# Split weights placed first in SBUF, and identity transposes in five chunks of a two-layer encoder kernel

## Chip, cores and metric

The kernel runs on one core of a Trainium2 chip. The metric is the device time of one execution in microseconds. The kernel is given as the median of several runs; one further execution was taken by the hardware profiler, and every trace number comes from that one.

## What is computed

A trunk of two layers over 256 tokens of width 2048, in fp32. Each layer is a norm, a token mixer, a residual add, a norm, a gated MLP with a depthwise convolution of width 3, a residual add. Layer 0 mixes with a bidirectional mLSTM of 8 heads, layer 1 with a bidirectional gated linear recurrence (HGRN2) of 16 heads.

```python
def conv_glu(hn, w_up, conv_w, conv_b, w_down):
    u = hn @ w_up                                   # 2048 -> 2 x 5504
    a, v = jnp.split(u, 2, axis=-1)
    ...                                             # c: a convolved over 3 tokens
    return (jax.nn.gelu(c, approximate=False) * v) @ w_down

def reference(x, ...):
    h = x
    for layer in range(DEPTH):
        hn = rmsnorm(h, norm_mix_g[layer])
        if layer % N_MIXERS == 0:
            mix = mlstm_mixer(hn, ...)              # p = hn @ w_in -> q, k, v, o, gates; y @ w_out
        else:
            mix = hgrn_mixer(hn, ...)               # p = hn @ w_in -> q, i, g, f_f, f_b; y @ w_out
        h = h + mix
        h = h + conv_glu(rmsnorm(h, norm_ffn_g[layer]), ...)
    return rmsnorm(h, final_g)
```

## The kernel before

**Products in three parts.** All large products run on TensorE as fp32r. A weight tile `raw` comes from memory, ScalarE rounds it to `wh` (L144) and VectorE takes the rest, `wl = raw - wh` (L145). Activations are split in the same way; a tile `x` of 128 features holds the high half of 256 tokens in its columns 0 to 255 and the low half in 256 to 511. A product is wh with x high, wh with x low, and wl with x high.

**Chunks.** The whole program is one list of chunks that `stream` works off in order. A chunk is a strip of a weight matrix with all `nk` tiles of the contraction dimension, and accumulates in two PSUM banks `ps`. There are two main kinds:

- "fm" (feature-major, 256 weight columns): the weights are stationary and x moves. For each k and each of the two halves f there is one pair: L199 moves all 512 columns of x past wh, L200 moves the first 256 past wl. A chunk of 16 k has 32 pairs. The q and k projections of the mLSTM, the q and gate projections of the HGRN and the up projections of the MLP are of this kind.
- "tm" (token-major, 512 weight columns): x is stationary and the weights move. For each k and each of the two token halves t there are three products of 512 columns: L189 (x high, wh), L190 (x high, wl), L191 (x low, wh). The v, o, g and all output and down projections are of this kind. L176 to L178 are the same for the very last chunk.

The first chunk mixes both kinds (L189 to L194).

**The order of the chunks.** In the mLSTM, for each of four pairs of heads `pr`: v (tm), q (fm), k (fm), o (tm), and then four chunks of the output projection (tm). The MLP is cut in two parts: 22 up chunks (fm), four down chunks (tm), 21 up chunks (fm), four down chunks (tm). The HGRN has for each of four groups of heads three fm chunks, v, three fm chunks, g, and then its output projection.

**Side work.** The attention parts, and the transposes that bring the residual stream into feature-major form for the next norm (`Norm.turn`, L268), are generators that `Side` steps between the products. Their short matmuls therefore stand among the pairs of the fm chunks. They write to a ring of four PSUM banks, handed out by `aux`. `Norm.turn` runs in the chunks that follow an output projection with a norm behind it: the first up chunk of each layer's first part, and the first chunks of the HGRN. Behind the down projection of a first part nothing is pushed.

**Where tiles lie.** A tile pool takes its place in SBUF in the order in which pools are opened, and its tiles lie in the order in which they are first asked for. `keep` comes first (parameters, constants with the identity `ident`, the residual stream hx, the 16 tiles xt, the 16 tiles yt, which hold ya, yb and g0 to g15 in turn), then `wpool` (three raw, four wh, four wl), then `ev`, and then the pools of the stages; the MLP's pool holds g16 to g21. The instructions are put in order by the tile framework with a timeline model; in both kernels the order on every engine is that of the source but for this scheduling.

Of the kernel before, what the change touches and what calls it, by code (L numbers as in the profile page):

```python
# [9 lines left out]
F32R = mybir.dt.float32r  # L10
# [5 lines left out]
P = 128  # L16
T = 256
D = 2048
KT = D // P
# [24 lines left out]
WB = 4  # L44
# [8 lines left out]
def trunk_kernel(ctx, tc, xT, x_d, fg_d, pp_d, cst_d, w_first, w_aq, w_ak, w_av, w_ao, w_aout,  # L53
                 w_bq, w_bv, w_bg, w_bout, w_up, w_down, out, mscr):
    nc = tc.nc
    act, dve, pool, pe = nc.scalar, nc.vector, nc.gpsimd, nc.tensor

    keep = ctx.enter_context(tc.tile_pool(name="keep", bufs=1))
    wpool = ctx.enter_context(tc.tile_pool(name="wpool", bufs=1))
    ev = ctx.enter_context(tc.tile_pool(name="ev", bufs=1))  # L60
# [11 lines left out]
    ident = cst[:, C_ID:C_ID + P]  # L72
# [5 lines left out]
    def aux(name):  # L78
        return psa.tile([P, 512], F32, tag="aux", name=name)


    class Side:
        def __init__(self):
            self.now, self.jobs = 0.0, []
# [26 lines left out]


    class Chunk:
        def __init__(self, kind, src, nk, x, done, before=None, last=False):
            self.last = last
            self.kind, self.src, self.nk, self.x, self.done, self.before = kind, src, nk, x, done, before
            self.width = {"fm": 256, "tm": 512, "first": 512 + P}[kind]

    def split_weights(chunks):

        first = True
        for ch in chunks:
            total = ch.nk * ch.width
            cuts = [0]
            if first:
                cuts = [k * ch.width for k in FIRST]
            while cuts[-1] < total:
                cuts.append(min(total, cuts[-1] + 2048))
            step = ch.width if first else 1024
            for b0, b1 in zip(cuts, cuts[1:]):  # L130
                n = b1 - b0
                raw = wpool.tile([P, 2048], F32, tag="raw", bufs=RAW, name="raw")
                nc.sync.dma_start(raw[:, :n], ch.src[:, b0:b0 + n])
                if first:
                    k0, k1 = b0 // ch.width, b1 // ch.width
                    (nc.scalar if k0 < 2 else nc.sync).dma_start(hx[:, k0:k1], xT[:, k0:k1])
                    if k0 == 0:
                        nc.scalar.dma_start(pp[:, 0:KT], pp_d[:, 0:KT])
                for c0 in range(0, n, step):
                    m = min(step, n - c0)  # L140
                    wh = wpool.tile([P, 1024], F32R, tag="wh", bufs=WB, name="wh")
                    wl = wpool.tile([P, 1024], F32R, tag="wl", bufs=WB, name="wl")
                    r = raw[:, c0:c0 + m]
                    act.copy(wh[:, :m], r)  # L144
                    dve.tensor_tensor(wl[:, :m], r, wh[:, :m].bitcast(F32), ALU.subtract)  # L145
                    yield wh, wl, m // ch.width
            first = False

    def stream(chunks):
        pieces = split_weights(chunks)  # L150
        ready = []

        def fetch():
            p = next(pieces, None)
            if p is not None:
                ready.append(p)

        for _ in range(LOOK):
            fetch()
        for ch in chunks:  # L160
            if ch.before:
                ch.before()
            ps = [psm.tile([P, 512], F32, tag="mm", name="mm") for _ in range(3 if ch.kind == "first" else 2)]
            k = 0
            while k < ch.nk:
                fetch()
                wh, wl, n = ready.pop(0)
                if ch.last and k + sum(p[2] for p in ready) + n == ch.nk:
                    pieces_, k0 = [(wh, wl, n)] + ready, k
                    for t in range(2):  # L170
                        k = k0
                        for wh, wl, n in pieces_:
                            for kk in range(n):
                                x, c = ch.x(k), slice(kk * 512, (kk + 1) * 512)
                                xh, xl = x[:, t * P:(t + 1) * P], x[:, T + t * P:T + (t + 1) * P]
                                pe.matmul(ps[t], xh, wh[:, c], start=False, stop=False)  # L176
                                pe.matmul(ps[t], xh, wl[:, c], start=False, stop=False)
                                pe.matmul(ps[t], xl, wh[:, c], start=False, stop=k == ch.nk - 1)  # L178
                                k += 1
                        ch.half(ps[t], t)  # L180
                    return
                for kk in range(n):
                    x = ch.x(k)
                    st, sp = k == 0, k == ch.nk - 1
                    if ch.kind != "fm":
                        c = slice(kk * 512, (kk + 1) * 512)
                        for t in range(2):
                            xh, xl = x[:, t * P:(t + 1) * P], x[:, T + t * P:T + (t + 1) * P]
                            pe.matmul(ps[t], xh, wh[:, c], start=st, stop=False)  # L189
                            pe.matmul(ps[t], xh, wl[:, c], start=False, stop=False)  # L190
                            pe.matmul(ps[t], xl, wh[:, c], start=False, stop=sp)  # L191
                        if ch.kind == "first":
                            pe.matmul(ps[2], wh[:, 512:512 + P], x, start=st, stop=False)
                            pe.matmul(ps[2][:, 0:T], wl[:, 512:512 + P], x[:, 0:T], start=False, stop=sp)  # L194
                        side.tick(1.3)
                    else:
                        for f in range(len(ps)):
                            c = kk * ch.width + f * P
                            pe.matmul(ps[f], wh[:, c:c + P], x, start=st, stop=False)  # L199
                            pe.matmul(ps[f][:, 0:T], wl[:, c:c + P], x[:, 0:T], start=False, stop=sp)  # L200
                        side.tick(0.325 * len(ps))
                    k += 1
            ch.done(ps)
# [179 lines left out]
    def mlstm(norm, nxt):  # L383
# [150 lines left out]
        chunks = []  # L534
        for pr in range(AH // 2):
# [41 lines left out]
                chunks.append(Chunk("first", w_first, KT, first_x, done_first, begin))  # L577
            else:
                chunks.append(Chunk("tm", w_av[pr - 1], KT, norm.x, done_v))
            chunks.append(Chunk("fm", w_aq[pr], KT, norm.x, done_q))  # L580
            chunks.append(Chunk("fm", w_ak[pr], KT, norm.x, done_k))
            chunks.append(Chunk("tm", w_ao[pr], KT, norm.x, done_o))

# [196 lines left out]
    def ffn(layer, norm, nxt):  # L780
        stack = ExitStack()
        box = {}
        chunks = []

        def begin():
            box["mp"] = stack.enter_context(tc.tile_pool(name="ff", bufs=1))
            if isinstance(nxt, FinalNorm):
                nxt.begin(box["mp"])

        def done_up(f, i, GT):  # L790
            def go(ps):
                mp, R = box["mp"], norm.R
                a = mp.tile([P, T], F32, tag="a", bufs=2, name="a")
                v = mp.tile([P, T], F32, tag="v", bufs=2, name="v")
                c = mp.tile([P, T], F32, tag="c", bufs=2, name="c")
                fm_scaled(ps[0], R, a)
                fm_scaled(ps[1], R, v)
                cw = [col("conv_w", (layer * 3 + w) * FT + f) for w in range(3)]
                dve.tensor_scalar(c, a, cw[1], col("conv_b", layer * FT + f), ALU.mult, ALU.add)
                dve.scalar_tensor_tensor(c[:, 1:T], a[:, 0:T - 1], cw[0], c[:, 1:T], ALU.mult, ALU.add)  # L800
                dve.scalar_tensor_tensor(c[:, 0:T - 1], a[:, 1:T], cw[2], c[:, 0:T - 1], ALU.mult, ALU.add)
                act.activation(c, c, AF.Gelu)
                dve.tensor_tensor(c, c, v, ALU.mult)
                g = slot(i, "g", mp)
                act.copy(g[:, 0:T], c)
                dve.tensor_tensor(g[:, T:2 * T], c, g[:, 0:T].bitcast(F32), ALU.subtract)
                GT.append(g)
            return go

        for part, (f0, nf) in enumerate(((0, FA), (FA, FB))):  # L810
            GT = []
            for i in range(nf):
                chunks.append(Chunk("fm", w_up[layer, f0 + i], KT, norm.x, done_up(f0 + i, i, GT),
                                    begin if f0 + i == 0 else None))
            chunks += project(lambda c: w_down[layer, c][:, f0 * 512:(f0 + nf) * 512], nf,
                              lambda k, GT=GT: GT[k], nxt if part else None)
        return chunks, stack.close
# [11 lines left out]
    chunks = mlstm(n0, n1)  # L829
# [95 lines left out]
```

## Time and profile before

| | |
|---|---|
| median of 3 runs | 2473.72 us (2473.66 to 2474.13) |
| the profiled execution | 2473.85 us |
| its span, first to last instruction | 2472.1 us |
| L199, 512 columns, fm | 3776 |
| L200, 256 columns, fm | 3776 |
| L189, L190, L191, 512 columns, tm | 1442 each |
| L268, transposes of 128 columns | 96 |
| mean granted TensorE clock | 0.999 |

The busy time of a matmul in the trace overlaps with that of the next, since matmuls are pipelined; what a matmul costs is read from its start to the start of the next. The trace keeps starts in whole nanoseconds; the timeline view prints them to 0.01 us.

### The profile page before, as it was taken

The page shows a single profiled execution, that of the slowest core. Times are in us where ns is not written, and L with a number is a line of the kernel's source. Part 1 is how long each engine was busy: PE and PEld are TensorE (multiplying, and loading weights), DVE is VectorE, ACT ScalarE, POOL GpSimd, SP SyncE. Part 2 cuts the span into 40 slices and gives each one's busy share as a digit, 9 for nine tenths or more (in the row PEclk, how much of TensorE's full clock was granted, in tenths as well). Part 3 has the DMA queues.
Part 4 walks back from the last instruction along what each step waited for, and adds up shares of the span by engine and source line. Part 5 has one row for each costly group of instructions (what it writes and reads, how often), then busy time and mean ns, then how long its engine had stood idle before and what let it go on. Part 6 is the DMA issues. An engine that isn't in the chain of part 4 may idle for free.

```text
span 2472.1 us, 33659 instructions
## 1 busy us (share of the span) xinstructions
PE 2459.1 (99%) x13032; PEld 2102.3 (85%) x13032; DVE 1719.2 (70%) x2816; ACT 1188.3 (48%) x1751; POOL 153.4 (6%) x235
## 2 busy tenths in 40 slices
PE   9999999999999999999999999999999999999998
PEld 7888888888888888888888888888888888888887
DVE  7766656777645777657888888895677754677754
ACT  6555455454434444445444444445544543444443
POOL 0100000000000000002212222220000000000000
PEclk9999999999999999999999999999999999999999
DMA  7654555555555555555444444445555555655554
GB/s 287 198 175 170 179 176 188 188 189 190 192 190 193 188 188 187 171 187 186 163 156 168 154 165 157 156 154 205 187 188 188 190 185 189 203 186 185 186 186 143
DMA packets 66192, 452.06 MB, mean 183 GB/s; under 512 B 7648, under 2 KB 8032, under 8 KB 13424
## 3 DMA queue, kind: packets, MB, share of 16 engines
q1 hardware_dynamic: 63792, 443.29, 53.4%
q0 software_dynamic: 1232, 5.31, 0.8%
q8 instruction: 102, 1.67, 0.3%
q10 hardware_dynamic: 1008, 1.32, 0.1%
q14 instruction: 58, 0.48, 0.1%
HBM read 447.72 MB, written 2.16 MB: 182 GB/s over the span
## 4 chain that ended last, share of the span: by engine, by line
PE 93%; DVE 5%; issue 1%; ACT 1%; DMA 0%; SPq 0%; POOLq 0%; POOL 0%; DVEq 0%
PE mm L199 34%; PE mm L200 17%; PE mm L190 12%; PE mm L191 12%; PE mm L189 12%; DVE wl L145 2%; PE pd L688 2%; DVE QK L689 1%; PE pn L499 1%; DVE km L671 1%; PE py L713 1%; PE pz L268 0%; DVE AT L666 0%; DVE qm L671 0%; ACT wh L144 0%
## 5 line engine op out<-in xcount | busy, mean ns | idle before, releaser
L145 DVE TENSOR_TENSOR wl<-raw,wh 128x1024 fp32r<-128x1024 f32 (+1 forms) x848 | 1030.5, 1216 | 608.9 <-ACT wh L144 600.4
L199 PE MATMUL mm<-xt,wh 128*128 128x512 f32 x3776 | 1329.5, 397 | 0.0
L144 ACT CAST wh<-raw 128x1024 fp32r<-128x1024 f32 (+1 forms) x848 | 881.7, 1041 | 925.7 <-PE mm L191 441.5
L200 PE MATMUL mm<-xt,wl 128*128 128x256 f32 x3776 | 1056.5, 280 | 0.0
L199 PEld LDWEIGHTS mm<-xt,wh 128*128 128x128 f32 x3776 | 708.6, 188 | 166.0
L200 PEld LDWEIGHTS mm<-xt,wl 128*128 128x128 f32 x3776 | 711.8, 188 | 1.2
L191 PE MATMUL mm<-wh,g 128*128 128x512 f32 x674 | 263.9, 392 | 0.0
L189 PE MATMUL mm<-wh,g 128*128 128x512 f32 x674 | 263.6, 391 | 0.0
L190 PE MATMUL mm<-wl,g 128*128 128x512 f32 x674 | 263.4, 391 | 0.0
L189 PE MATMUL mm<-wh,xt 128*128 128x512 f32 x512 | 203.6, 401 | 1.8 <-ACT xt L206 1.8
L190 PE MATMUL mm<-wl,xt 128*128 128x512 f32 x512 | 204.4, 399 | 0.4 <-DVE wl L145 0.4
L191 PE MATMUL mm<-wh,xt 128*128 128x512 f32 x512 | 202.6, 397 | 0.0
L211 ACT COPY b<-mm 128x256 f32<-128x256 f32 x237 | 87.9, 371 | 183.6 <-PE mm L200 183.6
L191 PEld LDWEIGHTS mm<-wh,g 128*128 128x128 f32 x674 | 126.6, 188 | 27.5
L190 PEld LDWEIGHTS mm<-wl,g 128*128 128x128 f32 x674 | 126.6, 188 | 27.2
L189 PEld LDWEIGHTS mm<-wh,g 128*128 128x128 f32 x674 | 126.6, 188 | 27.2
L189 PEld LDWEIGHTS mm<-wh,xt 128*128 128x128 f32 x512 | 96.1, 189 | 20.3 <-ACT xt L206 2.1
L190 PEld LDWEIGHTS mm<-wl,xt 128*128 128x128 f32 x512 | 97.0, 189 | 18.5 <-DVE wl L145 0.8
L191 PEld LDWEIGHTS mm<-wh,xt 128*128 128x128 f32 x512 | 97.0, 189 | 18.0
L212 DVE TENSOR_TENSOR a<-mm,b 128x256 f32<-128x256 f32 x86 | 36.5, 425 | 54.8 <-ACT b L211 54.8
L688 PEld LDWEIGHTS pd<-qm,km 128*128 128x128 f32 x448 | 62.9, 191 | 10.2 <-PE mm L191 4.2
L688 PE MATMUL pd<-qm,km 128*128 128x128 f32 x448 | 66.1, 276 | 1.2 <-DVE qm L671 1.1
(200 smaller groups left out, 1933.9 us busy)
## 6 DMA issues: line engine op xcount, KB each, us to landing
raw<-in_w_up SPq DMA_DIRECT2D x172, 1024.0 KB, 5.0
raw<-in_w_down SPq DMA_DIRECT2D x80, 1024.0 KB, 4.8
raw<-in_w_bq SPq DMA_DIRECT2D x48, 1024.0 KB, 5.0
raw<-in_w_ao SPq DMA_DIRECT2D x16, 1024.0 KB, 4.9
raw<-in_w_aout SPq DMA_DIRECT2D x16, 1024.0 KB, 4.8
raw<-in_w_bv SPq DMA_DIRECT2D x16, 1024.0 KB, 5.0
raw<-in_w_bg SPq DMA_DIRECT2D x16, 1024.0 KB, 4.8
raw<-in_w_bout SPq DMA_DIRECT2D x16, 1024.0 KB, 4.9
```

What stands on the lines that cost most here:

```text
L144: act.copy(wh[:, :m], r)
L145: dve.tensor_tensor(wl[:, :m], r, wh[:, :m].bitcast(F32), ALU.subtract)
L189: pe.matmul(ps[t], xh, wh[:, c], start=st, stop=False)
L190: pe.matmul(ps[t], xh, wl[:, c], start=False, stop=False)
L191: pe.matmul(ps[t], xl, wh[:, c], start=False, stop=sp)
L199: pe.matmul(ps[f], wh[:, c:c + P], x, start=st, stop=False)
L200: pe.matmul(ps[f][:, 0:T], wl[:, c:c + P], x[:, 0:T], start=False, stop=sp)
L211: act.copy(b, ps[:, T:2 * T])
L212: dve.tensor_tensor(dst, ps[:, 0:T], b, ALU.add)
L499: pe.matmul(pn[:, 0:258], w, v, start=(i == 0), stop=(i == len(parts) - 1))
L671: dve.tensor_copy(m.rearrange("k (m p j) -> k m p j", p=2, j=h), blocks(z, h, 0, T))
L688: pe.matmul(pd[:, c], km[:, c], qm[:, c], start=True, stop=True)
```

## The change

There are two edits, and the new code is all in the diff.

- A new pool `split`, opened before all others, holds the eight tiles wh and wl. They were in `wpool`, behind raw. In bytes of a partition:

| tiles | before | after |
|---|---|---|
| wh, wl | 132160 to 148543, 148544 to 164927 | 16512 to 32895, 32896 to 49279 |
| xt0 to xt15 | 42048 to 74815 | 74816 to 107583 |
| yt0 to yt15 (ya, yb, g0 to g15) | 74816 to 107583 | 107584 to 140351 |
| raw | 107584 to 132159 | 140352 to 164927 |
| ev and the stages' pools (g16 to g21 from 179584 in layer 0, from 187840 in layer 1) | | the same |

- A chunk can have `turns`. In an fm chunk, ahead of the products of k = 2, that many transposes of the identity into one bank of the ring `aux` are issued. Nothing reads the result. The q chunks of the head pairs 0 to 3 get 0, 4, 2 and 1; the first up chunk of the second MLP part gets 1 in layer 0 and 4 in layer 1. All other chunks get none.

On each engine the instructions and their order are otherwise those of the kernel before; TensorE has 12 more.

```diff
+    split_pool = ctx.enter_context(tc.tile_pool(name="split", bufs=1))
     keep = ctx.enter_context(tc.tile_pool(name="keep", bufs=1))
...
-        def __init__(self, kind, src, nk, x, done, before=None, last=False):
-            self.last = last
+        def __init__(self, kind, src, nk, x, done, before=None, last=False, turns=0):
+            self.last, self.turns = last, turns
...
-                    wh = wpool.tile([P, 1024], F32R, tag="wh", bufs=WB, name="wh")
-                    wl = wpool.tile([P, 1024], F32R, tag="wl", bufs=WB, name="wl")
+                    wh = split_pool.tile([P, 1024], F32R, tag="wh", bufs=WB, name="wh")
+                    wl = split_pool.tile([P, 1024], F32R, tag="wl", bufs=WB, name="wl")
...
                     else:
+                        if k == 2 and ch.turns:
+                            it = aux("turns")
+                            for i in range(ch.turns):
+                                pe.transpose(it[:, i * P:(i + 1) * P], ident, ident)
                         for f in range(len(ps)):
...
-            chunks.append(Chunk("fm", w_aq[pr], KT, norm.x, done_q))
+            chunks.append(Chunk("fm", w_aq[pr], KT, norm.x, done_q, turns=(0, 4, 2, 1)[pr]))
...
                 chunks.append(Chunk("fm", w_up[layer, f0 + i], KT, norm.x, done_up(f0 + i, i, GT),
-                                    begin if f0 + i == 0 else None))
+                                    begin if f0 + i == 0 else None,
+                                    turns=(4 if layer else 1) if part and i == 0 else 0))
```

## The prediction

> **What bounds the kernel now.** I read the page first: the engines, the granted clock, the chain of waits.
>
> ```profile
> span 2472.1 us, 33659 instructions
> PE 2459.1 (99%) x13032; PEld 2102.3 (85%) x13032; DVE 1719.2 (70%) x2816; ACT 1188.3 (48%) x1751; POOL 153.4 (6%) x235
> PEclk9999999999999999999999999999999999999999
> PE 93%; DVE 5%; issue 1%; ACT 1%; DMA 0%; SPq 0%; POOLq 0%; POOL 0%; DVEq 0%
> ```
>
> TensorE is never without work, its clock is full throughout, and 93% of the chain is its own. So the time is a sum of start-to-start steps of matmuls, and an edit is worth what it does to those steps. Next I put four stretches of 200 us side by side (busy us and counts by engine, then clock and DMA). All four hold up chunks alone: first part of layer 0, second part of layer 0, and the same of layer 1.
>
> ```profile
> core 0: us, PE busy (x) PEld busy (x) DVE busy (x) ACT busy (x) POOL busy (x), PEclk, DMA share, GB/s
> 414.00:614.00 200.00, 200.00 (x1156) 174.90 (x1155) 146.63 (x236) 100.91 (x147) 0.00 (x0) 1.00 0.58 190
> 780.00:980.00 200.00, 200.00 (x1135) 173.50 (x1134) 143.72 (x231) 96.78 (x141) 0.00 (x0) 1.00 0.56 184
> 1760.00:1960.00 200.00, 200.00 (x1155) 174.92 (x1154) 147.58 (x237) 100.09 (x146) 0.00 (x0) 1.00 0.58 190
> 2120.00:2320.00 200.00, 200.00 (x1134) 173.44 (x1133) 144.40 (x232) 96.83 (x142) 0.00 (x0) 1.00 0.57 187
> ```
>
> The same instructions at the same clock, yet the second parts get 21 matmuls fewer through. A pair (L199 with 512 columns, L200 with 256) is the unit. The second part of layer 0 starts at 767.25 us and its successor at 1004.69: 237.44 us for 21 x 32 = 672 pairs, **353.3 ns** a pair. The first part between 410.41 and 646.51 runs 681 pairs at **346.7 ns**. These two paces are all there is: over every fm run of the trace the mean settles on one or the other and stays, whichever wh or wl buffer is in use and whatever ACT, DVE and DMA do. How a stretch comes to its pace is in the timeline (start, duration, line). It is the q chunk of the second head pair, behind x-stationary products:
>
> ```profile
> 112.73 0.39 PE L191 MATMUL mm<-wh,xt 128*128 128x512 f32 x1
> 112.96 0.39 PE L199 MATMUL mm<-xt,wh 128*128 128x512 f32 x1
> ...
> 113.30 0.40 PE L199 MATMUL mm<-xt,wh 128*128 128x512 f32 x1
> ...
> 113.65 0.40 PE L199 MATMUL mm<-xt,wh 128*128 128x512 f32 x1
> ...
> 114.01 0.40 PE L199 MATMUL mm<-xt,wh 128*128 128x512 f32 x1
> ```
>
> Pair lengths 340, 350, 361 ns, and then 350, 361, 349 round and round: mean 353.3. All five stretches that come so, with nothing but products before them (q and k of head pairs 1 to 3, the two second up parts), stay in this cycle to their end. A stretch that something short breaks into can leave it:
>
> ```profile
> 1125.66 0.28 PE L200 MATMUL mm<-xt,wl 128*128 128x256 f32 x1
> 1125.78 0.40 PE L199 MATMUL mm<-xt,wh 128*128 128x512 f32 x1
> 1126.01 0.28 PE L200 MATMUL mm<-xt,wl 128*128 128x256 f32 x1
> 1126.13 0.27 PE L268 MATMUL pz<-cst,hx 128*128 128x128 f32 x1
> 1126.16 0.48 PE L199 MATMUL mm<-xt,wh 128*128 128x512 f32 x1
> 1126.47 0.28 PE L200 MATMUL mm<-xt,wl 128*128 128x256 f32 x1
> 1126.59 0.39 PE L199 MATMUL mm<-xt,wh 128*128 128x512 f32 x1
> 1126.82 0.28 PE L200 MATMUL mm<-xt,wl 128*128 128x256 f32 x1
> ```
>
> Before the one transpose this stretch goes 350, 361; behind it, after one long pair, 347, 347. The step ahead of the transpose is 236 ns from L199 to L200, the same that stands at the end of the fourth pair of the five stretches (114.01 to 114.25).
>
> **The transposes.** The five chunks get 4, 2, 1 (q of pairs 1 to 3) and 1, 4 (up) transposes, 12 in all, each ahead of k = 2, so behind the fourth pair; order of instructions on all engines is otherwise unchanged. *Cost:* from the last L200 before one transpose to the second L199 behind it the trace has 578 ns (1126.01 to 1126.59) against 116 + 347 = 463 in steady pace, 0.115 us. Around a burst of four at 406.29 us it is 905 against 463, 0.442 us. So 0.115 x 2 + 0.442 x 2 + about 0.22 for the two = **1.3 us**, all on the path, since nothing of TensorE's is hidden. They read only the identity and nobody reads their bank; the waits on the three q bursts are for TensorE's own earlier products. *Gain,* if all five change pace: an up part has 668 pairs left, 668 x 6.67 ns = 4.45 us, twice 8.9; q and k together 60 pairs, 0.40 us, three times 1.2. Sum **10.1 us**. Whether each does change: the case above has one transpose at the same phase and leaves the slow cycle; bursts of four at 406.4 and 1750.3 us, behind a step of 235 ns, leave it too (the next pairs are 346, 347). For two transposes at this phase there is no row: of three cases in attention with two, all entering at the fast pace, one stayed fast and two fell to 353.3. I take all five as changing, and keep none as the other end. What is late next if they speed up: nothing, because the first parts run 346.7 with the same ACT, DVE and DMA work a pair and no idle TensorE. Net **-8.8 us**.
>
> [...]
>
> **The move.** It changes no instruction and no order; in bytes of a partition, by the tiles' sizes in the order of the pools, wh and wl go from 132160-164927 to 16512-49279, xt from 42048 up to 74816-107583, yt to 107584-140351, raw to 140352-164927. If places matter, it is in rows like these, where the stationary tile passes from g15 (105536) to g16 (179584) under the same moving wh and wl:
>
> ```profile
> 758.40 0.39 PE L190 MATMUL mm<-wl,g 128*128 128x512 f32 x1
> 758.63 0.39 PE L191 MATMUL mm<-wh,g 128*128 128x512 f32 x1
> 758.85 0.40 PE L189 MATMUL mm<-wh,g 128*128 128x512 f32 x1
> 759.09 0.39 PE L190 MATMUL mm<-wl,g 128*128 128x512 f32 x1
> ```
>
> Steps of 226 and 227 turn to 236 and 230 at once, and all 498 steps on g16 to g21 average 232.9, all on g2 and g5 to g15 226.7: **6.2 ns** a matmul. That is a matter of place, and no row tells which: the far end as such, or how the two tiles lie to each other. For the far end as such, the boundary lies above 164927: the first pair behind x-stationary products (112.96) loads wh and wl at 132160 and 148544 in 227 and 113 ns, nothing lost; the 256-column step loses as much with a near tile behind it (135.45 us, xt0 next: 113, then 233, 236) as with wh. Then nothing that moves crosses the boundary. Bounds: -25.2 us (all 3776 pairs come to 340 ns, as the first does) and +23.8 us (3840 x-stationary products that now step 226.7 go to 232.9). I take **0**, by the 227 and 113 ns.
>
> **Sum.** 2473.85 (the profiled execution: span 2472.07, 1.78 around it) - 8.8 = 2465.05; that execution is 0.13 above the median, so **2464.9 us**.
>
> **Rivals.** *(a) Some or all bursts miss.* One up part left slow costs 4.45: 2469.4. [...] For it: half of the attention's bursts of short matmuls end at 353.3. Against: the three transpose bursts at or near this phase. I give 0.12 to some missing and 0.06 to none changed.
> *(b) The low place frees the pairs.* 340 ns everywhere: 2464.9 - 25.2 = 2439.7; half of it 2452. For it: 340 does occur, and low stationary tiles step evenly. Against: the 256-column step falls out of step with near and far tiles alike.
> *(c) Slower: x-stationary products lose their even step.* Now wh and wl lie below every stationary tile, as they do below g16 to g21 today; if that order is what costs 6.2 ns, 3840 products pay 23.8: 2488.7. It decides from 8.8 / 0.0062 = 1420 products on, 37%. Against: stationary wh above moving xt loses nothing in its first pair.
>
> **How the numbers follow.** Forecast 0.52, (a) 0.18, (b) 0.15, (c) 0.15. Alone the likeliest would be 2463 to 2468 (only q bursts missing adds 1.2). The range goes down to (b) whole and up past none changed: **2438 to 2478**; outside it is (c) and the rest of (b). 0.2% is 4.9 us, so below 2468.8 is faster: forecast, (b) and a little of (a), 0.69; (a) otherwise 0.16 within; (c) 0.15 slower.
>
> **What would show it.** The windows 780 to 980 and 2120 to 2320 should count about 1155 matmuls as the first parts do, and pairs behind each burst 346 and 347 ns. A count of 1135 in one: (a), and which burst. Over 1170 in the first parts too: (b). Steps of 231 and 236 on xt or g0 to g15: (c). Idle TensorE ahead of L199 there would show that splits are late.

## Result: slower, and by another mechanism than the forecast's

The changed kernel takes 2491.67 us (median of 4 runs, 2491.49 to 2491.69) beside 2473.81 us for the kernel before (4 runs, 2473.66 to 2474.13). The ratio is 1.0072, with a 95% interval of 1.0054 to 1.0089. The forecast was 2464.9 us and its range ended at 2478.

The page of the changed kernel, in the lines that were read before: span, engines, granted clock, and the chain of waits by engine.

```profile
span 2489.9 us, 33683 instructions
PE 2475.5 (99%) x13044; PEld 2108.5 (85%) x13044; DVE 1719.4 (69%) x2816; ACT 1187.5 (48%) x1751; POOL 153.4 (6%) x235
PEclk9999999999999999999999999999999999999999
PE 96%; DVE 2%; issue 1%; ACT 0%; DMA 0%; SPq 0%; POOLq 0%; POOL 0%; DVEq 0%
```

The kernel is still bound by TensorE at full clock (mean granted clock 0.999 in both kernels), with 12 matmuls more, and still without gaps: VectorE's share of the chain of waits even fell from 5% to 2%. So the 17.8 us that the span grew (2489.9 less 2472.1) are again in the steps from one matmul's start to the next. The same four windows of 200 us, of the changed kernel (busy us and counts by engine, then clock, DMA share and GB/s):

```profile
414.00:614.00 200.00, 200.00 (x1134) 173.70 (x1133) 144.45 (x232) 98.05 (x143) 0.00 (x0) 1.00 0.57 187
780.00:980.00 200.00, 200.00 (x1134) 173.69 (x1134) 142.21 (x226) 96.87 (x141) 0.00 (x0) 1.00 0.57 186
1760.00:1960.00 200.00, 200.00 (x1136) 173.83 (x1135) 142.72 (x229) 99.07 (x145) 0.00 (x0) 1.00 0.57 186
2120.00:2320.00 200.00, 200.00 (x1126) 173.32 (x1125) 139.58 (x218) 94.85 (x136) 0.00 (x0) 1.00 0.57 188
```

The second parts were to come up to 1155 matmuls. Instead the first parts fell from 1156 and 1155 to 1134 and 1136: all four are now at the slow pace. (The last window begins some 7 us before its up part, whose first products now start at 2126.7 us; that is where its further 8 matmuls went.) In the timeline, in the second up part of layer 0 and well behind its transpose, three pairs take 1.06 us, 353 ns each (the line shown is the 512-column product of a pair, L204 in this kernel):

```profile
777.11 0.40 PE L204 MATMUL mm<-xt,wh 128*128 128x512 f32 x1
...
778.17 0.40 PE L204 MATMUL mm<-xt,wh 128*128 128x512 f32 x1
```

It is not the old slow cycle. Before, the 512-column steps went 233, 241, 236 and the 256-column steps 117, 120, 113; now, once a stretch has settled, every 512-column step is 235 ns and every 256-column step 118 or 119, in every fm stretch of the kernel, and neither a burst nor a `Norm.turn` leads out of it. Start-to-start steps summed by kind, in us:

| steps | before | after | difference |
|---|---|---|---|
| fm, 512 and 256 columns | 1335.0 | 1349.1 | +14.1 |
| tm on g0 to g15, ya, yb | 526.4 | 532.4 | +6.1 |
| tm on g16 to g21 | 122.7 | 121.2 | -1.5 |
| tm on xt | 366.4 | 364.9 | -1.6 |
| short matmuls, the transposes among them | 111.6 | 112.3 | +0.8 |

Each number is rounded by itself; unrounded, the differences add up to the 17.8 us. Of the xt row, steps under 260 ns went from 228.7 to 229.7 ns on the mean, and the time beyond 227 ns in the longer ones fell by 2.9 us (15.3 to 12.4). Of that time, 8.3 us before and 8.2 after lie in steps under 340 ns, nearly all of them right behind a short matmul; the fall is in the longest steps. That goes with VectorE's smaller share of the chain, as if a slower TensorE waited less for VectorE, but no run shows it to be the cause.

### The profile page after: what moved, and what is told of

The parts are those of the page before. It is cut to its first block, busy times and chain, and to the rows that moved or that the text cites. A ratio compares the mean times of both kernels' runs of the same rounds, so it can differ in the third digit from the quotient of the medians.

```text
span 2489.9 us, 33683 instructions
## 1 busy us (share of the span) xinstructions
PE 2475.5 (99%) x13044; PEld 2108.5 (85%) x13044; DVE 1719.4 (69%) x2816; ACT 1187.5 (48%) x1751; POOL 153.4 (6%) x235
## 4 chain that ended last, share of the span: by engine, by line
PE 96%; DVE 2%; issue 1%; ACT 0%; DMA 0%; SPq 0%; POOLq 0%; POOL 0%; DVEq 0%
PE mm L204 35%; PE mm L205 18%; PE mm L191 13%; PE mm L192 13%; PE mm L190 13%; PE pd L693 2%; DVE wl L146 1%; PE pn L504 1%; PE py L718 1%; PE pz L273 0%; DVE QK L694 0%; PE S L490 0%; DVE km L676 0%; DMA raw<-in_w_first 0%; PE pd L683 0%
## 5 line engine op out<-in xcount | busy, mean ns | idle before, releaser
L204 PE MATMUL mm<-xt,wh 128*128 128x512 f32 x3776 | 1341.7, 398 | 0.0
L204 PEld LDWEIGHTS mm<-xt,wh 128*128 128x128 f32 x3776 | 709.9, 188 | 170.7
```

## What the experiments tell apart

The places in bytes suggest a new theory. A tile's place is taken modulo 256 bytes, which is an assumption that a shift by 256 tries further below, and the place of the moving tile is taken from that of the stationary tile:

| products | before | after |
|---|---|---|
| fm (wh or wl stationary, x moves) | 64 - 64 = **0** | 128 - 64 = **64** |
| tm on xt, ya, yb, g0 to g15 (x stationary) | **0** | 64 - 128 = **192** |
| tm on g16 to g21, layer 0 | 128 - 64 = **64** | 128 - 128 = **0** |
| tm on g16 to g21, layer 1 | 192 - 64 = **128** | **64** |

The theory says that the step of a matmul hangs on this difference alone. Its rival in the first runs is the far place as such, high or low in SBUF, as the prediction had it for g16 to g21. The median of the kernel before was between 2473.60 and 2473.68 us beside all the runs that follow.

### The two edits, each alone

The transposes alone, with wh and wl at their old place:

```diff
...
+                        if k == 2 and ch.turns:
+                            it = aux("turns")
+                            for i in range(ch.turns):
+                                pe.transpose(it[:, i * P:(i + 1) * P], ident, ident)
...
-            chunks.append(Chunk("fm", w_aq[pr], KT, norm.x, done_q))
+            chunks.append(Chunk("fm", w_aq[pr], KT, norm.x, done_q, turns=(0, 4, 2, 1)[pr]))
...
-                                    begin if f0 + i == 0 else None))
+                                    begin if f0 + i == 0 else None,
+                                    turns=(4 if layer else 1) if part and i == 0 else 0))
```

> The 12 transposes alone, wh and wl in their old place. The prediction's step on the transposes: if all five stretches leave the 353.3 ns cycle for 346.7, about 2465 us, and 200 us windows in the second up parts count some 1155 matmuls; each up part that stays slow adds 4.45. Rival, that a burst changes nothing there either, as in the changed kernel: 2475.

Measured: 2474.81 us, ratio 1.0005 (0.9995 to 1.0014). The bursts bring next to nothing: of the five chunks only the q chunk of the last head pair changes pace. Its burst of one (timeline of this kernel, where the transpose is L200 and the pairs are L203 and L204):

```profile
261.71 0.27 PE L200 MATMUL turns<-cst 128*128 128x128 f32 x1
261.73 0.47 PE L203 MATMUL mm<-xt,wh 128*128 128x512 f32 x1
...
262.16 0.39 PE L203 MATMUL mm<-xt,wh 128*128 128x512 f32 x1
...
262.51 0.39 PE L203 MATMUL mm<-xt,wh 128*128 128x512 f32 x1
```

Behind it the steps are 230 and 117 ns to the end of the chunk and through the k chunk that follows it. The second up part of layer 0 gets the same single transpose:

```profile
769.13 0.27 PE L200 MATMUL turns<-cst 128*128 128x128 f32 x1
769.16 0.48 PE L203 MATMUL mm<-xt,wh 128*128 128x512 f32 x1
...
769.59 0.40 PE L203 MATMUL mm<-xt,wh 128*128 128x512 f32 x1
...
769.95 0.40 PE L203 MATMUL mm<-xt,wh 128*128 128x512 f32 x1
```

The steps into the two bursts differ by no more than a nanosecond (241, 120, 236, then 120 in the first and 119 in the second), the first long step behind is 314 ns in both, and yet here it goes 240, 120, 236, 114 again.

The move alone (the new pool is opened ahead of all others, as in the changed kernel):

```diff
...
+    split_pool = ctx.enter_context(tc.tile_pool(name="split", bufs=1))
...
-                    wh = wpool.tile([P, 1024], F32R, tag="wh", bufs=WB, name="wh")
-                    wl = wpool.tile([P, 1024], F32R, tag="wl", bufs=WB, name="wl")
+                    wh = split_pool.tile([P, 1024], F32R, tag="wh", bufs=WB, name="wh")
+                    wl = split_pool.tile([P, 1024], F32R, tag="wl", bufs=WB, name="wl")
```

> The move alone, no added transpose. If the whole loss belongs to the move and the bursts only cost their own 1.3 us there: about 2490.3, with every pair at 353.3 and the x-stationary steps at 229 to 233. If bursts and move do harm together: near 2474.

Measured: 2490.17 us, ratio 1.0069 (1.0052 to 1.0086), 16.6 us above the kernel before (2473.61). With the transposes' 1.50 us (2491.67 less 2490.17) that is the whole result, to 0.2 us. In the steps: fm +12.3, tm on g0 to g15, ya and yb +6.1, on g16 to g21 -1.5.

### Far place or difference of places

Two kernels cross the theories. The first moves wh and wl to the front, but with gaps of 960 bytes ahead of them and 1088 behind, so that every difference, and every tile's own place modulo 256, is as before the change:

```diff
+    gap0 = ctx.enter_context(tc.tile_pool(name="gap0", bufs=1))
+    gap0.tile([P, 240], F32, name="gap0")
+    split_pool = ctx.enter_context(tc.tile_pool(name="split", bufs=1))
+    gap1 = ctx.enter_context(tc.tile_pool(name="gap1", bufs=1))
+    gap1.tile([P, 272], F32, name="gap1")
```

> wh and wl first in SBUF as in the changed kernel, no transposes, but with a gap of 960 bytes ahead of them and one of 1088 behind them, so that wh, wl, xt and yt all have the old remainder again (64 of 512, 1088 of 2048). Theory offset (the difference of the places of stationary and moving tile, modulo 256 bytes, sets the steps): as before, 2473.8, pairs at 346.7 and 353.3, x-stationary steps 226.7. Theory place (low wh and wl under higher stationary tiles cost 6 ns a step): as the move alone, about 2490.

The second keeps the old order and puts only 64 bytes between raw and wh:

```diff
+    gap = ctx.enter_context(tc.tile_pool(name="gap", bufs=1))
+    gap.tile([P, 16], F32, name="gap")
+    spool = ctx.enter_context(tc.tile_pool(name="spool", bufs=1))
...
-                    wh = wpool.tile([P, 1024], F32R, tag="wh", bufs=WB, name="wh")
-                    wl = wpool.tile([P, 1024], F32R, tag="wl", bufs=WB, name="wl")
+                    wh = spool.tile([P, 1024], F32R, tag="wh", bufs=WB, name="wh")
+                    wl = spool.tile([P, 1024], F32R, tag="wl", bufs=WB, name="wl")
```

> The old order of the pools, no transposes, with a gap of 64 bytes between raw and wh: wh and wl lie 64 bytes higher, everything else TensorE reads in the long products where it was. Theory offset: as the move alone, about 2490, all pairs at 353.3, x-stationary steps 229 to 233. Theory place: as before, 2473.8.

At the front with the old differences: 2473.71 us, ratio 1.0000 (0.9991 to 1.0010). At the old place plus 64 bytes: 2491.64 us, ratio 1.0072 (1.0057 to 1.0087). The first up parts of the two, in the windows view:

```profile
414.00:614.00 200.00, 200.00 (x1156) 174.84 (x1155) 146.84 (x236) 101.02 (x147) 0.00 (x0) 1.00 0.58 190
```

```profile
414.00:614.00 200.00, 200.00 (x1135) 173.72 (x1134) 144.32 (x232) 98.20 (x143) 0.00 (x0) 1.00 0.57 188
```

1156 matmuls in the far move, 1135 with the gap. The far place as such does nothing here; 64 bytes bring the whole loss. By the order of the pools the 64 bytes also move what lies behind wh and wl, g16 to g21 among it, although the expectation put down above says that all else stays. Their difference is therefore kept, and so is their step (233.1 ns, 232.9 before). The move alone had gained 1.5 us there, and that is how far 2491.64 lies above 2490.17.

The same products in the changed kernel tell the difference from a tile's own place modulo 256. g16 to g21 have not moved, and only wh and wl have come from 64 to 128. In layer 0, where both tiles now are at 128, the steps went from 233.3 to 227.0 ns; in layer 1 the stationary tile is at 192, the difference is 64, and they are 233.0. So for tm a difference of 0 goes with 227.0 ns and one of 64 with 233.0 to 233.3, at each of the places seen here. For the pairs nothing here tells the two apart: in every kernel x stays at 64, and only the weights are moved.

The products on g16 to g21 are the other end of it: the same theory says that their 6.2 ns can be had back by moving g16, far as it is, until the difference is 0.

```diff
+            box["mp"].tile([P, 32 if layer else 48], F32, name="gap")
```

> The kernel before with a gap of 192 bytes (layer 0) and 128 bytes (layer 1) ahead of g16, so that g16 to g21 lie at 64 modulo 256 as wh and wl do. Theory offset: their 528 products step 226.7 and not 232.9, 3.3 us less, 2470.4. Theory that the far end of SBUF costs: 2473.7.

Measured: 2470.17 us, ratio 0.9986 (0.9977 to 0.9995). Steps on g16 to g21 went from 232.9 to 226.7 ns, 3.3 us over 527 of them, without moving nearer to the front. In the timeline five steps on g16 take 1.13 us; the five from 758.85 us on in the kernel before took 1.17:

```profile
758.23 0.39 PE L190 MATMUL mm<-wl,g 128*128 128x512 f32 x1
...
759.36 0.39 PE L189 MATMUL mm<-wh,g 128*128 128x512 f32 x1
```

### How the pace goes with the difference

In the next kernels the tiles wh and wl are 4352 bytes long (17 x 256, where they were 4096), and fm chunks alone use them shifted, so that only fm changes:

```diff
+FM_OFF = 32
...
-                    wh = wpool.tile([P, 1024], F32R, tag="wh", bufs=WB, name="wh")
-                    wl = wpool.tile([P, 1024], F32R, tag="wl", bufs=WB, name="wl")
+                    o = FM_OFF if ch.kind == "fm" else 0
+                    wh = wpool.tile([P, 1088], F32R, tag="wh", bufs=WB, name="wh")[:, o:o + 1024]
+                    wl = wpool.tile([P, 1088], F32R, tag="wl", bufs=WB, name="wl")[:, o:o + 1024]
```

`FM_OFF` is in columns of 4 bytes: 32 gives a difference of 128 bytes, and 48, 64, 8 and 56 give 192, 256, 32 and 224.

> fm chunks alone read wh and wl 128 bytes higher inside their tiles (which grow by 256 bytes); tm chunks read them where they were. Theory that only a difference of 0 modulo 256 runs well: pairs at 353.3 flat, x-stationary steps 226.7, about 2486 us. Rival, that the fm pairs have a best difference of their own (before, only a start in step lasted two products at difference 0): pairs nearer 340, down to 2441.

> The same with 192 bytes (64 modulo 256 on the other side). Zero-is-best theory: pairs at 353.3 flat, about 2486. Rival of a best difference elsewhere: pairs nearer 340, down to 2441. If 64 to one side and 64 to the other are alike, as at f128 or not, the sign of the difference does not count.

> The same with 256 bytes. Period of 256 bytes: as before, 2473.7 within 1 us (which stretches are at 346.7 and which at 353.3 may differ). A longer period: another pace.

> The same with 32 bytes. If the grain is 64 bytes or more, as before, 2473.7; if the pace changes with any difference, pairs at one flat pace between 340 and 353.3, so 2441 to 2486.

> fm chunks read both 224 bytes higher, 32 short of a full period. If the sign of the difference does not count: as with 32, cycles of 353.3 and 346.7, about 2483. If it does, as it did at 192 against 64: a cycle of its own, between 346.7 and 353.3.

A last one of this kind shifts wl alone by 128 bytes, so that of a pair only the 256-column product's stationary tile has moved:

```diff
+                    wh = wpool.tile([P, 1088], F32R, tag="wh", bufs=WB, name="wh")[:, 0:1024]
+                    wl = wpool.tile([P, 1088], F32R, tag="wl", bufs=WB, name="wl")[:, o:o + 1024]
```

> fm chunks read wl alone 128 bytes higher, wh at difference 0. If each step follows the difference between the moving x and the tile loaded during it: L199 (wl is loaded) as with both at 128, mean 231.8 in place of 235.2, L200 (wh is loaded) as before, 116.9; some 12 us less, 2461. If the pair only works as a whole: another cycle, anywhere from 2441 to 2486.

| fm difference, bytes | time, us | ratio (interval) | pace of pairs, ns |
|---|---|---|---|
| 0 (before) | 2473.6 | | 346.7 or 353.3 |
| 32 | 2482.94 | 1.0035 (1.0019 to 1.0051) | 353.3, a few stretches 346.7 |
| 64 (place of the change, move alone) | 2490.17 | 1.0069 (1.0052 to 1.0086) | 353.3 only |
| 128 | 2477.30 | 1.0014 (1.0003 to 1.0026) | 351.1 |
| 192 | 2477.91 | 1.0016 (1.0005 to 1.0027) | 348.9 or 353.3 |
| 224 | 2462.37 | 0.9953 (0.9937 to 0.9969) | 346.7 only, once settled |
| 256 | 2473.74 | 0.9999 (0.9988 to 1.0010) | 346.7 or 353.3 |
| wh 0, wl 128 | 2470.20 | 0.9985 (0.9975 to 0.9996) | 346.7 or 350.0 |

In the row of 64 the tm products are at 192, too; in all others they are as before. 256 is 0 again, to the pace (2473.74 us beside 2473.68 for the kernel before), so the longer tiles cost nothing by themselves. Of the shifts tried 256 alone brings back the time and both paces, as a period of 256 bytes would; 128 (2477.30 us), 64 (2490.17) and 32 (2482.94) do not. The distance from 0 doesn't settle it either, since 32 and 224 (32 bytes to the other side) are 20.6 us apart.

Two expectations missed. At 128 and 192 the time was to be about 2486 if only 0 ran well, and lower if another value had pairs near 340 ns; 2477.30 and 2477.91, at 351.1 and at 348.9 or 353.3, are neither. With wl alone shifted it was to be 2461 if each step followed the tile that is loaded during it; 2470.20, at 346.7 or 350.0, speaks for a pace that belongs to the pair as a whole.

224 was the surprise: the theory gave the period and not the order of the values, and 224 came out below both kernels. The windows view of it, first and second part of layer 0 and second part of layer 1:

```profile
414.00:614.00 200.00, 200.00 (x1156) 177.30 (x1156) 147.44 (x236) 100.63 (x147) 0.00 (x0) 1.00 0.58 190
780.00:980.00 200.00, 200.00 (x1155) 177.33 (x1154) 146.37 (x236) 98.91 (x145) 0.00 (x0) 1.00 0.58 190
...
2120.00:2320.00 200.00, 200.00 (x1155) 177.30 (x1155) 146.36 (x236) 98.60 (x144) 0.00 (x0) 1.00 0.59 190
```

All are at 1155 or 1156, what the transposes were to bring to the second parts, and it takes no transpose: in steady pace the steps are 228 or 229 and 118 or 119 ns in every stretch.

### Bursts once more

With g16 aligned, the steps ahead of both second up parts are even (227 ns), as they are ahead of the q chunk whose single transpose worked. The kernel with that gap, one transpose ahead of each second part's k = 2, and 1, 3 and 6 in the q chunks:

```diff
-            chunks.append(Chunk("fm", w_aq[pr], KT, norm.x, done_q))
+            chunks.append(Chunk("fm", w_aq[pr], KT, norm.x, done_q, turns=(0, 1, 3, 6)[pr]))
...
-                                    begin if f0 + i == 0 else None))
+                                    begin if f0 + i == 0 else None,
+                                    turns=1 if part and i == 0 else 0))
...
+            box["mp"].tile([P, 32 if layer else 48], F32, name="gap")
```

> b1 with bursts again: one transpose in both second up parts and in the q chunk of head pair 1, three in that of pair 2, six in that of pair 3. With g16 to g21 aligned, all five stretches start in step, as the q chunk did in which one transpose worked. If start and number decide: both up parts at 346.7, 2470.4 - 8.9 + 0.2 = about 2461.7, and the chunk with one transpose fast. If the outcome hangs on something finer than that: some of the three with one transpose stay at 353.3, and the time lies between 2461.7 and 2471.6.

Measured: 2471.23 us, ratio 0.9990 (0.9980 to 1.0000), so 1.06 us above the kernel with the gap alone: the cost of its 12 transposes less a small gain. The burst of six changed the pace of its q chunk and the k chunk behind it, to pairs of 350 and 343 or 344 in turn, 346.7 on the mean. Both second up parts went back to 241, 120, 236, 113 behind a transpose entered with 241, 120, 236, 119 and left with a step of 314. Of the five single transposes in the two kernels the one that worked had 120 ns as its last step ahead and the four others 119; the one at 1126.13 us that led out of the slow cycle in the kernel before had 120 as well. But the burst of four in the q chunk of the second head pair, in the first of the two kernels, had 120, too, and changed nothing. The trace keeps whole nanoseconds, so what decides may lie below one, or in something that the trace doesn't hold; that stays open.

### The sign, and a faster kernel

Left open were whether 224 is good by itself or through the products ahead of the pairs, and whether x-stationary products have such a value, too. The first kernel is that of 224 with the gap ahead of g16; the second shifts wh and wl in every chunk (`o = FM_OFF`), by which tm on xt, ya, yb and g0 to g15 comes to 32.

> f224 (the up, q, k and HGRN products read wh and wl 224 bytes higher, so that the stationary tile lies 224 bytes above the moving one, modulo 256) together with the gap of b1 ahead of g16 (192 B in layer 0, 128 B in layer 1). Theory that each product's step hangs on its own two tiles' places modulo 256 alone: the two gains add up, f224's 2462.4 us less b1's 3.3 to 3.5 us gives 2458.9 to 2459.1, g16-g21 steps 226.7 ns and all pairs 346.7 ns. Rival, that the pace a pair run takes hangs on how the products before it ended (as it does at difference 0): with the down products before them changed, some pair runs fall back to 353.3 ns and the time lies between 2459 and 2469 us.

> As f224, but the x-stationary products too read wh and wl 224 bytes higher, so that there the stationary tile lies 32 bytes above the moving one modulo 256 (in f224: 0). Theory that only the difference modulo 256 counts and that x-stationary products are best at 0: their even steps of 226.7 ns go to 229-233 ns, on the 3456 steps of xt, g0-g15, ya and yb that are 8 to 22 us, 2470 to 2484 us. Rival, that a difference of 32 bytes either way is as good as 0 for them: 2462 us, as f224.

The first: 2458.75 us (2458.54 to 2458.94), ratio 0.9939 (0.9924 to 0.9953), all pairs at 346.7 ns and all steps on g16 to g21 at 226.7. The two gains add up, to 0.2 us (11.2 and 3.4 less apart, 14.9 less together). The chain of waits on its page:

```profile
PE 90%; DVE 7%; issue 1%; ACT 1%; DMA 0%; POOL 0%; SPq 0%; POOLq 0%; DVEq 0%
```

The order of instructions is that of the kernel before. VectorE's share of the chain is 7%, where it was 5%; the weight split has 2% of it in both kernels, and the other lines of VectorE that the page lists there are those of the attention. It is the fastest of all kernels run here, and 32.9 us below the changed one.

The second: 2481.23 us, ratio 1.0031 (1.0019 to 1.0043). Its pairs are at 346.7 ns as before, but the tm steps under 260 ns went to 233.2 (xt), 233.3 (g0 to g15) and 233.3 (ya, yb). g16 to g21, which come to 96 in layer 0 and to 160 in layer 1, are at 234.2 and 233.3. For tm the mean steps by difference, over all these kernels and without xt, are 226.7 to 227.6 (0; 226.7 in even stretches), 233.3 (32), 233.0 to 233.3 (64), 234.2 (96), 232.5 to 233.1 (128), 233.3 (160) and 229.1 to 230.1 (192); 0 is the best of those seen. The difference sets them to about 1 ns, and what makes up the rest was not looked into.

## Why the prediction was wrong

**What bounds the kernel** was right, and so was the unit of account: start-to-start steps at full clock. The pairs at 346.7 or 353.3 ns are there in every kernel with difference 0.

**"The move. ... I take 0"** is the step that failed, and the larger one: it costs 16.6 us by itself. It was bounded at -25.2 and +23.8, and the value in between was taken from one row, the first pair behind x-stationary products, at 227 and 113 ns. That row cannot price the move: in it, as in every pair of the kernel before, the difference is 0, and the only long products of that kernel with another difference are those on g16 to g21, at 6.2 ns. The sentence ahead of it had named the right alternative, "the far end as such, or how the two tiles lie to each other", and the working then went on with the far end alone. The places in bytes that the prediction lists show that the move changes the second: wh goes from 132160, which is 64 modulo 256, to 16512, which is 128, while xt and yt stay at 64.

**"I take all five as changing"** failed, too. At the old place one of five changed, the q chunk of the last head pair and with it the k chunk, 60 pairs x 6.7 ns = 0.4 us, against 10.1 us. Of the rows it rested on only one, the single transpose at 1126.13 us, shows a settled slow cycle being left. Ahead of the bursts of four at 406.4 and 1750.3 us stand just two pairs, of 435 and 355 ns, behind another burst, so there was no cycle to leave. And the same trace has bursts that failed: at 1285.29, 1418.16 and 1550.83 us four short products of the attention break into the slow cycle behind its step of 235 or 236 ns, after 46 pairs of it, and it goes on behind one long pair. Before the burst of 1285.29 the pairs are 349, 350 and 361 ns in turn, behind it 348, 361, 349, 350. In the changed kernel it came true nowhere: at a difference of 64 no stretch settled at another pace than 353.3 ns, there, in the move alone and with the gap of 64 bytes. Rival (a) is nearly right for the transposes alone: with none changed the kernel before and their 1.3 us make 2475.0, and 2474.81 was measured with one changed.

**The transposes' own cost** was nearly right: 1.3 us forecast; 1.6 measured at the old place (2474.81 less 2473.61 is 1.2, with those 0.4 gained back) and 1.5 in the changed kernel.

**Rival (b)**, the low place frees the pairs, fell: with the old differences the low place is worth nothing (2473.71). That pairs *can* all be faster is right, but by the difference (224) and at 346.7 ns, not at 340.

**Rival (c)** was nearest in time, 2488.7, and has the right row, the steps on g16 to g21. Its mechanism, wh and wl lying below every stationary tile, fell with the far move that cost nothing, so the time is near by luck. What it named is only the smaller part: even steps on xt, g0 to g15, ya and yb were lost, as it said, but they went to 229.1 to 230.1 ns and not to 232.9. In the move alone g0 to g15, ya and yb cost 6.1 us and xt next to nothing, where it had 23.8 for all of them, and 12.3 us came from the pairs, which it left out.

In time, 64 bytes between raw and wh are worth 18.0 us (2491.64 against 2473.61). What in the chip makes the two places count, no run here shows.

## What to carry to other kernels

Where TensorE sets the time, compute for each kind of product the place of the stationary tile less that of the moving one modulo 256 bytes, before and after any edit that allocates, moves or resizes a tile; an edit that looks free can shift it for every product behind it, and here 64 bytes of padding cost 18.0 us. Where both operands come from pools, a few bytes of padding can set it, separately for each kind of product; here that was worth 14.9 us, with 224 for weights that are stationary and 0 for x that is, the best of the values tried in this kernel. When a pace is kept for a whole stretch, find what sets it before putting instructions in to break it: the 12 transposes cost 1.6 us at the old place and brought 0.4 back.

## What was not expected of the hardware

- In these kernels the start-to-start steps of back-to-back fp32r matmuls went with the difference of the two tiles' places modulo 256 bytes: 226.7 to 234.2 ns for 512 columns with x stationary, 346.7 to 353.3 ns for a pair of 512 and 256 columns. For the pairs it may be the place of the weights by itself, since x was never moved modulo 256.
- The sign counts for the pairs: with their weights 32 bytes up the kernel takes 2482.94 us, and with 224, which is 32 down modulo 256, 2462.37.
- At a difference of 0 the pairs ran at two lasting paces, 346.7 and 353.3 ns, and 1 of 5 bursts put between them in one kernel and 1 of 5 in another changed the pace, for a reason that the steps in whole nanoseconds don't show. At 64, 128 and 224 the settled stretches had one pace: 353.3, 351.1 and 346.7 ns.
- Shifting wl alone by 128 bytes gives 350.0 ns for most pairs, a pace that no shift of both gave.
